# RWKV-7 score products of two heads issued in turn, with a PSUM bank for each head

## The chip, the cores and the metric

The kernel runs as one program on one core of a Trainium2 chip. The metric is the device time of one execution in microseconds (us). The kernel before was run three times; every run of a kernel executes the whole program.

## The reference, cut to what matters

The program is a network of several blocks on one sequence of 512 tokens. The change lies in the third block, in its RWKV-7 branch: 8 heads of 64 channels, whose state is a 64 x 64 matrix per head.

```python
def rwkv7_scan(r, decay, k, v, a, b):
    """S_t = S_{t-1} diag(decay_t) + (S_{t-1} a_t) b_t^T + v_t k_t^T ; y_t = S_t r_t. Inputs (B,T,H,N)."""
    ...
def rwkv7_time_mix(pb, mu, w0, w2, a0, a2, g2, k_k, k_a, r_k, lnx_w, lnx_b):
    ...
    kk = l2_normalize(heads(k * f32(k_k)))
    k = k * (1.0 + (a - 1.0) * f32(k_a))
    r, k, v, a, decay = heads(r), heads(k), heads(v), heads(a), heads(decay)
    y = rwkv7_scan(r, decay, k, v, -kk, kk * a)
    ...
```

## The kernel before, in words

The kernel does not step through the 512 tokens. It cuts them into 4 chunks of 128 and works on a pair of heads at a time (`p` = 0 to 3, heads 2p and 2p + 1). Channels lie on the 128 rows of a tile: the first head of a pair on rows 0 to 63, the second on rows 64 to 127. A pair passes through three functions:

- `rwkv_a` (line 1958) prepares the pair: r, k and v mixed with the token before, the normalized key kk (the norm is the matmul at line 1819, followed by ScalarE at 1820 and 1821 and VectorE at 1822), the gates, and the running sum of the log of the decay (a scan, line 1995, and what follows it to line 2006). It leaves `AR` (kk and r, scaled by the decay, two planes of 512 columns) and `B` and `Kb` (b and k, scaled by its inverse). Three more matmuls stand at its end: line 2024 (the bonus) and lines 2028 and 2029 (the output gate). Each uses the one bank "pa".
- `rwkv_b` (line 2033) makes the scores. For each source (`B`, then `Kb`), head and chunk, one matmul of 64 rows multiplies 128 columns of the source with 2 x 128 columns of `AR`; in all 16 matmuls per pair and 64 in the program, in float32. Two chunks of one head share a PSUM bank of the kind "mx". A copy under a mask (`copy_predicated`, VectorE, line 2047) brings the triangle of both chunks into a tile of zeros, `s8z`. There are two banks of the kind "mx", so at most two such groups are in flight. At its end `rwkv_b` calls `tri_inv` on the tile from `B`.
- `tri_inv` (line 1740) inverts 8 triangular matrices of 128 x 128. Blocks of 16 are done by substitution on VectorE (lines 1756 and 1757, fifteen rounds), VectorE transposes them (`iv_xc`, line 1759; `iv_yc`, line 1761), and TensorE doubles the blocks (from line 1769 on), with sums on VectorE (lines 1780, 1781) and copies on ScalarE (up to line 1812), in "mx" banks too.
- `rwkv_d` (line 2051) runs the recurrence over the four chunks with these scores and the inverse (lines 2066 to 2085), one chunk after another, then a layer norm.

The other branch of the block, a gated delta rule, has functions of the same kind (`gdn_b`, its recurrence at lines 1927 to 1941), which use `tri_inv` and the same banks. Large projections (lines 325 to 327, three matmuls of 512 columns for each 128 x 128 block of weights, which VectorE splits into two parts at line 312 and ScalarE casts at line 310) and transposes by a matmul (line 1830) run through all of it.

The order of the work: a list names the pieces in the order in which they are emitted (`ra0` is `rwkv_a` of pair 0, `gb0` the `gdn_b` of pair 0), each is emitted as if it stood some hundred instructions earlier, by a table of priorities, and a scheduler in the framework then places every instruction on its engine by priority and readiness. It may take instructions of a later piece, or of another line, ahead.

```python
BANKS3 = {"pj": 3, "pa": 1, "mx": 2, "o": 1, "ad": 1}
PR3 = {"a": 0, "b": 400, "d": 500, "s": 300, "p": 150, "t": 300, "u": 0}
MIX3 = ("ra0 rb0 ra1 rd0 ga0 rb1 gb0 rd1 ra2 rb2 gd0 ga1 gb1 rd2 ra3 rb3 gd1 ga2 gb2 rd3 ga3 s0 s1 s2"
```

Of the kernel before, what the change touches and what calls it, by code (L numbers as in the profile page):

```python
# [37 lines left out]
# ---------------------------------------------------------------- host layout  # L38
# [5 lines left out]
def w_cols(w):  # L44
    """[K, C] -> [C/128, 128, K/128, 128]: one block of 128 columns per entry."""
    k, c = w.shape
    return w.reshape(k // P, P, c // P, P).transpose(2, 1, 0, 3)


def w_groups(w, kg, n=256):  # L50
    """[K, C] -> [K/(128 kg), C/n, 128, kg, n]: groups of kg k-tiles, n columns."""
    k, c = w.shape
    return w.reshape(k // (kg * P), kg, P, c // n, n).transpose(0, 3, 2, 1, 4)


def w_rows(w):
    """[K, C] -> [C/512, K/128, 128, 512]"""
    k, c = w.shape
    return w.reshape(k // P, P, c // 512, 512).transpose(2, 0, 1, 3)
# [20 lines left out]
def consts():  # L80
    """Constants that depend on shapes alone, [128, n] float32 each."""
# [9 lines left out]
    # block 2: rows of head h broadcast; causal masks [s, t]; distances [t, s]; compressed blocks [t, c]  # L91
# [25 lines left out]
def w_pick(w, blocks):  # L117
    """columns of w by index lists of 128 (None: a column of zeros) -> [n, 128, K/128, 128]"""
# [9 lines left out]
def layout(i):  # L128
    """numpy arrays of the reference -> arrays as the kernel reads them (moves only)."""
# [37 lines left out]
    w = i["hgrn_w_out"][0]                                           # heads 0-1, 2-5, 6-9, 10-13, 14-15  # L167
# [14 lines left out]
    fm = [rng(128 * m, 128) for m in range(4)]                       # 0: gu  # L182
    fm += [rng(1024 + 128 * m, 128) for m in range(8)]               # 4: mq, 8: mk
    fm += [rng(2560 + 128 * m, 128) for m in range(4)]               # 12: mo
    fm += [ui, uf]                                                   # 16
    fm += heads + [rng(a, 128) for a in (3848, 4104, 3592, 3720)]    # 18: nq, 22: nks, 23: nkw, 24: nkc, 25: nvc
    fm += [rng(4384 + 128 * m, 128) for m in range(24)]              # 26: ga, 34: gb, 42: gc
# [22 lines left out]
    fm = [rng(128 * m, 128) for m in range(16)]                      # 0: q, 4: k, 8: v, 12: z  # L210
    fm += [rng(r0 + 128 * m, 128) for m in range(12)]                # 16: r, 20: k, 24: v
    fm += [rng(r0 + 1536, 128), rng(r0 + 1664, 128), u2]             # 28: w_lo a_lo, 29: g_lo, 30: gates, g_lo
    fm += [rng(3888 + 128 * m, 128) for m in range(16)]              # 31: ga, 39: gb
# [17 lines left out]
# ---------------------------------------------------------------- helpers  # L231
def dview(t, off, dims):
    """A view of tile t with free strides of its own: dims = [[stride, count], ...]."""
# [3 lines left out]
class K:  # L237
# [39 lines left out]
    def banks(self, **n):  # L277
        """share the 8 banks of PSUM out to uses that do not wait for one another"""
# [7 lines left out]
    def tables(self, *after):  # L286
        """exp and ln on the scalar engine again, behind the instructions given, which need others"""
# [8 lines left out]
    def ahead(self, n):  # L296
        """schedule what is emitted inside as if it stood n instructions earlier"""
# [4 lines left out]
    # weights: load one unit and split it exactly into two float32r parts  # L302
# [12 lines left out]
    def split(self, hi, lo, src):  # L315
        """hi + lo = src exactly, both float32r."""
# [3 lines left out]
    def mm3(self, out, wpair, xpair, first, last):  # L320
        """out += w^T x with both operands in two parts (the product of the two low parts is
        below float32's rounding)."""
# [6 lines left out]
    def norms(self):  # L329
        """scratch of the norms below; opened before the work that precedes them"""  # L330
        return self.tc.tile_pool(name="nrm", bufs=2)
# [4 lines left out]
    def sums(self, tile, g=None):  # L336
        """add(k) takes tile k of the finished x into the sums of squares (with g, into those of (x g)^2 too);
        finish() returns the sums over all the channels"""
# [16 lines left out]
    def norm_x(self, pool, sums, A, B, g=None):  # L355
        """hh + hl = rms(x) * A + B; with g, x = rms(x) * g first. The sums of both norms are taken at once:
        mean((x r g)^2) = r^2 mean((x g)^2)."""
# [23 lines left out]
    def final(self, pool, sums, g, out):  # L381
        """out = rms(x) * g"""
# [10 lines left out]
    def mod(self, t, x, r, A, B, k, hi, lo):  # L393
        """hi + lo = x * r * A + B"""
# [5 lines left out]
    def rstd(self, pool, xs, n):  # L400
        """1 / sqrt(mean square over the channels of all tiles + eps)"""
# [14 lines left out]
    def layer_ab(self, ad, g, shift, scale, name):  # L416
        """A = (1 + scale) * g, B = shift of a modulated norm, [128, 8] each"""
# [4 lines left out]
    def softplus_neg_abs(self, out, x, bias=None):  # L422
        """out = log(1 + exp(-|x|))"""
# [8 lines left out]
    def logsig(self, out, x, sp):  # L432
        """out = log sigmoid(x) = min(x, 0) - sp, sp = log(1 + exp(-|x|))"""
# [12 lines left out]
    def silu_vec(self, names):  # L446
        """silu of vectors, side by side: [128, len, 8]."""
# [12 lines left out]
    def ada(self, w, cond, grp, bias, out, pool):  # L460
        """out[:, j, :] = (cond @ w)[block j] + bias for a group of 4 blocks of 128 columns, two conditions.
        cond [128, 4, 8]: the high and then the low parts of both."""
# [19 lines left out]
    def ada_later(self, w, cond, groups, bias, out):  # L482
        """the same for one condition, on the vector engine, in steps that other work takes along"""
# [22 lines left out]
    # ------------------------------------------------------------ block 1, layer 0  # L506
# [10 lines left out]
    def hgrn(self):  # L517
        nc, tc, I = self.nc, self.tc, self.I
        cond = self.cond1 = self.silu_vec(["c", "c_ctx"])
        with ExitStack() as st:  # L520
# [5 lines left out]
            with tc.tile_pool(name="hg_x", bufs=1) as xp, tc.tile_pool(name="hg_ar", bufs=16) as arp:  # L526
# [5 lines left out]
                # shift and scale of channels 0-511, then of the others  # L532
# [1598 lines left out]
```

## Time and profile before

| what | value |
|---|---|
| median of 3 runs | 3515.52 us |
| the runs | 3515.52, 3516.84, 3511.62 us |
| span of the profiled execution | 3510.5 us |
| TensorE busy in that span | 3380.7 us (96%) |
| VectorE busy | 2413.4 us (69%) |
| ScalarE busy | 1802.1 us (51%) |
| records of line 2046 | 128 matmuls, from 2542.1 to 2852.7 us |
| masked copies of line 2047 | 32, from 2544.2 to 2854.2 us |

For the profiled execution the span is known, and no time of its own; the three runs stand 1.1 to 6.3 us above this span. In the trace each float32 matmul is recorded twice, so the 64 matmuls of line 2046 are 128 records. The durations of matmul records are modelled at their end; a distance between two starts is safer. Clock columns give the granted clock of TensorE as a share of 2.4 GHz; 0.50 is 1.2 GHz. A time in a chain of waits is the share of the path, not the length of the instruction.

### The profile page before, as it was taken

To read this page: it belongs to the slowest core of one execution; us is meant where nothing else is said; L and a number is where in the kernel's file an instruction comes from. 1 tells how busy PE (TensorE), PEld (TensorE's weight loads), DVE (VectorE), ACT (ScalarE), POOL (GpSimd) and SP (SyncE) were. 2 spreads that over 40 slices of the span, in tenths; PEclk is the share of its full clock that TensorE was granted. 3 is DMA by queue.
4 is the path that set the end of the run, shared out by engine and by line. 5 is a ranking of instruction groups with operands and counts; after the bars stand their busy time and mean duration, and the time that the engine had idled before them with its cause. 6 is when DMAs were issued, how large, how long until landed. Compare 5 with 4: busy or idle time off the path is not lost.

```text
span 3510.5 us, 50868 instructions
## 1 busy us (share of the span) xinstructions
PE 3380.7 (96%) x20328; PEld 2686.3 (77%) x20328; DVE 2413.4 (69%) x3883; ACT 1802.1 (51%) x3000; POOL 123.6 (4%) x56
## 2 busy tenths in 40 slices
PE   7999999999799999999999999999899999999998
PEld 5888888888577777766787778888667667878887
DVE  6787767787689988466565465554757788565545
ACT  6556556466544565444455543334636556544434
POOL 0000000000132330000000000000000000000000
PEclk9999999999899999999999999999969999999999
DMA  6233323321121122333321235542201111323332
GB/s 224 88 102 95 100 91 100 106 79 55 49 72 61 66 78 95 123 108 108 93 79 58 86 120 180 186 157 96 102 21 45 34 43 37 105 88 96 96 96 84
DMA packets 109663, 325.10 MB, mean 93 GB/s; under 512 B 12721, under 2 KB 13361, under 8 KB 108786
## 3 DMA queue, kind: packets, MB, share of 16 engines
q1 hardware_dynamic: 109170, 321.06, 28.1%
q8 instruction: 160, 2.62, 0.3%
q0 software_dynamic: 256, 0.79, 0.1%
q14 instruction: 77, 0.63, 0.1%
HBM read 315.51 MB, written 6.29 MB: 92 GB/s over the span
## 4 chain that ended last, share of the span: by engine, by line
PE 78%; DVE 15%; ACT 4%; issue 2%; DMA 2%; POOL 0%; SPq 0%; DVEq 0%; ACTq 0%
PE ps_pj L326 19%; PE ps_pj L325 19%; PE ps_pj L327 19%; DVE w_lo L312 2%; DMA ada_raw<-ada_w 2%; DVE iv_m L1756 1%; PE ps_mx L1388 1%; PE ps_pj L1365 1%; PE ps_mx L2046 1%; PE ps_o L1394 1%; ACT w_hi L310 1%; DVE iv_xd L1757 1%; PE ps_ad L496 1%; PE ps_mx L326 1%; DVE cv_ul L318 1%
## 5 line engine op out<-in xcount | busy, mean ns | idle before, releaser
L325 PE MATMUL ps_pj<-hh,w_hi 128*128 128x512 f32 x2344 | 937.4, 401 | 19.8 <-ACT hh L397 18.9
L327 PE MATMUL ps_pj<-hh,w_lo 128*128 128x512 f32 x2344 | 935.0, 399 | 0.0
L326 PE MATMUL ps_pj<-hl,w_hi 128*128 128x512 f32 x2344 | 934.9, 399 | 0.0
L310 ACT CAST w_hi<-w_raw 128x1024 fp32r<-128x1024 f32 (+1 forms) x435 | 454.6, 1045 | 767.4 <-PE ps_pj L326 651.2
L312 DVE TENSOR_TENSOR w_lo<-w_raw,w_hi 128x1024 fp32r<-128x1024 f32 (+1 forms) x387 | 470.2, 1216 | 336.4 <-ACT w_hi L310 330.3
L325 PEld LDWEIGHTS ps_pj<-hh,w_hi 128*128 128x128 f32 x2344 | 445.9, 190 | 127.5 <-ACT hh L397 24.3
L326 PEld LDWEIGHTS ps_pj<-hl,w_hi 128*128 128x128 f32 x2344 | 446.0, 190 | 102.0 <-issue 12.9
L327 PEld LDWEIGHTS ps_pj<-hh,w_lo 128*128 128x128 f32 x2344 | 445.6, 190 | 101.3 <-issue 10.7
L493 DVE SCALAR_TENSOR_TENSOR ada_acc<-ada_raw,sv_t_c,ada_acc 128x512 f32<-128x512 f32 x224 | 167.4, 747 | 50.3 <-DMA ada_raw<-ada_w 48.5
L967 DVE SCALAR_TENSOR_TENSOR xT<-ps_pj,ad,xT 128x512 f32<-128x512 f32 x128 | 95.5, 749 | 153.8 <-PE ps_pj L327 153.3
L312 POOL TENSOR_TENSOR w_lo<-w_raw,w_hi 128x1024 fp32r<-128x1024 f32 x48 | 121.1, 2523 | 1175.5 <-ACT w_hi L310 1175.5
L909 DVE SCALAR_TENSOR_TENSOR ps_mx<-cv_ut,vec,ps_mx 128x448 f32<-128x448 f32 (+3 forms) x192 | 128.3, 669 | 1.9 <-PE ps_mx L327 1.0
L909 DVE SCALAR_TENSOR_TENSOR ps_ad<-cv_ut,vec,ps_ad 128x480 f32<-128x480 f32 (+2 forms) x192 | 128.5, 669 | 1.6 <-ACT ps_ad L898 0.5
L327 PE MATMUL ps_pj<-w_hi,hl 128*128 128x256 f32 x416 | 119.0, 288 | 2.5 <-DVE hl L398 2.5
L325 PE MATMUL ps_pj<-w_hi,hh 128*128 128x256 f32 x416 | 120.3, 290 | 0.8 <-ACT hh L397 0.6
L326 PE MATMUL ps_pj<-w_lo,hh 128*128 128x256 f32 x416 | 120.8, 291 | 0.0
L326 PE MATMUL ps_pj<-m_yl,w_hi 128*128 128x512 f32 x256 | 99.9, 390 | 0.0
L327 PE MATMUL ps_pj<-m_yh,w_lo 128*128 128x512 f32 x256 | 99.6, 389 | 0.0
L325 PE MATMUL ps_pj<-m_yh,w_hi 128*128 128x512 f32 x256 | 99.6, 389 | 0.0
L327 PEld LDWEIGHTS ps_pj<-w_hi,hl 128*128 128x128 f32 x416 | 80.7, 195 | 5.7 <-DVE hl L398 3.2
L325 PEld LDWEIGHTS ps_pj<-w_hi,hh 128*128 128x128 f32 x416 | 80.9, 194 | 3.6 <-ACT hh L397 1.2
L326 PEld LDWEIGHTS ps_pj<-w_lo,hh 128*128 128x128 f32 x416 | 80.8, 194 | 1.5 <-issue 0.7
(786 smaller groups left out, 6513.4 us busy)
## 6 DMA issues: line engine op xcount, KB each, us to landing
ada_raw<-ada_w SPq DMA_DIRECT2D x288, 256.0 KB, 2.8
w_raw<-w_in SPq DMA_DIRECT2D x97, 512.0 KB, 3.2
w_raw<-hgrn_w_in SPq DMA_DIRECT2D x64, 512.0 KB, 3.2
w_raw<-w_mlp SPq DMA_DIRECT2D x64, 512.0 KB, 3.3
w_raw<-conv_w_in SPq DMA_DIRECT2D x48, 512.0 KB, 3.2
w_raw<-w_ffn_in SPq DMA_DIRECT2D x44, 512.0 KB, 3.5
w_raw<-hgrn_w_v SPq DMA_DIRECT2D x16, 512.0 KB, 3.3
w_raw<-hgrn_w_out SPq DMA_DIRECT2D x16, 512.0 KB, 3.2
```

Of the source, the lines that this page charges most:

```text
L310: nc.scalar.copy(hi, raw)
L312: (nc.gpsimd if self.on_pool else nc.vector).tensor_tensor(lo, raw, hi.bitcast(F32), op=ALU.subtract)
L318: self.nc.vector.tensor_tensor(lo, src, hi.bitcast(F32), op=ALU.subtract)
L325: mm(out, wh, xh, start=first, stop=False)
L326: mm(out, wh, xl, start=False, stop=False)
L327: mm(out, wl, xh, start=False, stop=last)
L493: nc.vector.scalar_tensor_tensor(acc, raw, cond[:, k:k + 1], acc, op0=ALU.mult, op1=ALU.add)
L496: nc.tensor.matmul(col[:, b:b + 1], acc[:, 128 * b:128 * b + 128], self.c("ones")[:, 0:1], start=True, stop=True)
L909: stt(o, x, tap(j), o, op0=ALU.mult, op1=ALU.add)
L967: self.nc.vector.scalar_tensor_tensor(self.xT[:, m, :], acc, gate[:, m:m + 1], self.xT[:, m, :], op0=ALU.mult, op1=ALU.add)
L1365: mm(sc[:, :n], q[gs, 128 * i:n], ks[b][gs, 0:n], start=True, stop=True)
L1388: mm(banks[c // 512][:, c % 512:c % 512 + 128], p_[:, off[i] + 128 * s:off[i] + 128 * s + 128], dg[:, i, :], start=True, stop=True)
```

## The change

The loop over heads moves inside the loop over chunks. For a pair of chunks, a bank is taken for each of the two heads; the matmuls then alternate between the heads, and the two masked copies follow. The number of matmuls, of copies and of banks is the same. (Comments that the diff also strips are left out.) From here on the lines of the changed kernel are one or two higher: its matmuls are line 2047, its copies line 2049, and `rwkv_d` stands 2 lines later.

```diff
             o = self.s8z[2 if i else self.niv % 2]
-            for h in range(2):
-                hs = slice(64 * h, 64 * h + 64)
-                for c2 in range(0, 4, 2):
-                    sc = self.bank("mx", [P, 2, 2, P])
-                    for j in range(2):
-                        cs = slice(128 * (c2 + j), 128 * (c2 + j) + 128)
-                        mm(sc[:, j], src[hs, cs], AR[hs, :, cs], start=True, stop=True)
-                    nc.vector.copy_predicated(o[:, 4 * h + c2:4 * h + c2 + 2], self.tri2, sc)
+            for c2 in range(0, 4, 2):
+
+                scs = [self.bank("mx", [P, 2, 2, P]) for _ in range(2)]
+                for j in range(2):
+                    cs = slice(128 * (c2 + j), 128 * (c2 + j) + 128)
+                    for h in range(2):
+                        hs = slice(64 * h, 64 * h + 64)
+                        mm(scs[h][:, j], src[hs, cs], AR[hs, :, cs], start=True, stop=True)
+                for h in range(2):
+                    nc.vector.copy_predicated(o[:, 4 * h + c2:4 * h + c2 + 2], self.tri2, scs[h])
             out.append(o)
```

How the built programs differ follows at three places. In these rows "x2" is two such instructions in a row, and a tile's number tells one buffer from another of the same name: `ps_mx_21123` and `ps_mx_21124` are two banks.

**TensorE, pair 0.** The score products of pair 0 before (`ps_mx` with `rw_B` or `rw_K`, two of one head to a bank), with the matmul of line 2024 among them:

```order
L2046 MATMUL ps_mx_21123<-rw_AR_20927,rw_B_21081 128x256 x2
L2046 MATMUL ps_mx_21127<-rw_AR_20927,rw_B_21081 128x256 x2
L2024 MATMUL ps_pa_21115<-rw_r_21099,cst_b3_20722 128x512
L2046 MATMUL ps_mx_21131<-rw_AR_20927,rw_B_21081 128x256 x2
L2046 MATMUL ps_mx_21135<-rw_AR_20927,rw_B_21081 128x256 x2
L2046 MATMUL ps_mx_21139<-rw_AR_20927,rw_K_21082 128x256 x2
L2046 MATMUL ps_mx_21143<-rw_AR_20927,rw_K_21082 128x256 x2
L2046 MATMUL ps_mx_21147<-rw_AR_20927,rw_K_21082 128x256 x2
L2046 MATMUL ps_mx_21151<-rw_AR_20927,rw_K_21082 128x256 x2
```

and in the changed kernel, from the same instruction on:

```order
L2047 MATMUL ps_mx_21123<-rw_AR_20927,rw_B_21081 128x256
L2047 MATMUL ps_mx_21124<-rw_AR_20927,rw_B_21081 128x256
L2047 MATMUL ps_mx_21123<-rw_AR_20927,rw_B_21081 128x256
L2047 MATMUL ps_mx_21124<-rw_AR_20927,rw_B_21081 128x256
L2024 MATMUL ps_pa_21115<-rw_r_21099,cst_b3_20722 128x512
L2047 MATMUL ps_mx_21131<-rw_AR_20927,rw_B_21081 128x256
L2047 MATMUL ps_mx_21132<-rw_AR_20927,rw_B_21081 128x256
L2047 MATMUL ps_mx_21131<-rw_AR_20927,rw_B_21081 128x256
L2047 MATMUL ps_mx_21132<-rw_AR_20927,rw_B_21081 128x256
L2028 MATMUL ps_pa_21119<-s3_sg1_20862,rw_lw_20925 128x512
```

The two heads now alternate product by product, and lines 2024 and 2028 stand between the groups (line 2029 between the third and the fourth). Behind the last product came, before, the first steps of the recurrence (lines 2066, 2067), the gate and projections, and then the norm of pair 1 (line 1819):

```order
L2066 MATMUL ps_ad_21581<-rw_vt_21113,s8_2_20913 128x64
L2067 MATMUL ps_o_21580<-rw_vt_21113,s8_2_20913 128x64
L2028 MATMUL ps_pa_21119<-s3_sg1_20862,rw_lw_20925 128x512
L2066 MATMUL ps_ad_21581<-rw_vt_21113,s8_2_20913 128x64
L2067 MATMUL ps_o_21580<-rw_vt_21113,s8_2_20913 128x64
L2029 MATMUL ps_pa_21119<-s3_sg2_20780,rw_lw_20925 128x512
L326 MATMUL ps_pj_21717<-hl_92,w_hi_21713 128x512
L327 MATMUL ps_pj_21717<-hh_91,w_lo_21715 128x512
L325 MATMUL ps_pj_21717<-hh_91,w_hi_21713 128x512
L326 MATMUL ps_pj_21717<-hl_92,w_hi_21713 128x512
L1819 MATMUL ps_pa_21494<-rw_sq_21387,cst_b3_20722 128x512
```

and now, from the last group on:

```order
L2047 MATMUL ps_mx_21147<-rw_AR_20927,rw_K_21082 128x256
L2047 MATMUL ps_mx_21148<-rw_AR_20927,rw_K_21082 128x256
L2047 MATMUL ps_mx_21147<-rw_AR_20927,rw_K_21082 128x256
L2047 MATMUL ps_mx_21148<-rw_AR_20927,rw_K_21082 128x256
L2068 MATMUL ps_ad_21581<-rw_vt_21113,s8_2_20913 128x64
L2069 MATMUL ps_o_21580<-rw_vt_21113,s8_2_20913 128x64
L2068 MATMUL ps_ad_21581<-rw_vt_21113,s8_2_20913 128x64
L2069 MATMUL ps_o_21580<-rw_vt_21113,s8_2_20913 128x64
L1819 MATMUL ps_pa_21494<-rw_sq_21387,cst_b3_20722 128x512
L326 MATMUL ps_pj_21717<-hl_92,w_hi_21713 128x512
L327 MATMUL ps_pj_21717<-hh_91,w_lo_21715 128x512
```

The norm of pair 1 comes straight behind the recurrence's first steps, ahead of the projections. From the first score product of pair 0 up to the first matmul of its inverse (line 1769) there were 55 projection matmuls, and now there are 71.

**TensorE, pair 1.** The first score products of pair 1 (`rw_B_21538`), among steps of pair 0's recurrence, before:

```order
L2046 MATMUL ps_mx_21880<-rw_AR_21384,rw_B_21538 128x256
L2066 MATMUL ps_ad_21598<-rw_vt_21113,s8_2_20913 128x64 x2
L2069 MATMUL ps_ad_21598<-ch_S0_20909,rw_AR_20927 128x128
L2070 MATMUL ps_o_21580<-ch_S0_20909,rw_AR_20927 128x128
L2046 MATMUL ps_mx_21880<-rw_AR_21384,rw_B_21538 128x256
L2074 MATMUL ps_ad_21598<-rw_r_21605,iv_Y0_20906 128x64 x2
L2046 MATMUL ps_mx_21884<-rw_AR_21384,rw_B_21538 128x256
L2078 MATMUL ps_ad_21598<-rw_vt_21113,rw_kt_21097 128x128
L2079 MATMUL ps_ad_21598<-rw_u_21609,rw_bt_21090 128x128
L2085 MATMUL ps_o_21580<-rw_u_21609,s8_0_20911 128x64 x2
L2067 MATMUL ps_o_21580<-rw_vt_21113,s8_2_20913 128x64 x2
L2046 MATMUL ps_mx_21884<-rw_AR_21384,rw_B_21538 128x256
```

and now:

```order
L2047 MATMUL ps_mx_21880<-rw_AR_21384,rw_B_21538 128x256 x2
L2076 MATMUL ps_ad_21581<-rw_r_21586,iv_Y0_20906 128x64 x2
L2047 MATMUL ps_mx_21881<-rw_AR_21384,rw_B_21538 128x256
L2080 MATMUL ps_ad_21581<-rw_vt_21113,rw_kt_21097 128x128
L2081 MATMUL ps_ad_21581<-rw_u_21590,rw_bt_21090 128x128
L2087 MATMUL ps_o_21580<-rw_u_21590,s8_0_20911 128x64 x2
L2069 MATMUL ps_o_21580<-rw_vt_21113,s8_2_20913 128x64 x2
L2047 MATMUL ps_mx_21881<-rw_AR_21384,rw_B_21538 128x256
L2047 MATMUL ps_mx_21888<-rw_AR_21384,rw_B_21538 128x256
L2068 MATMUL ps_ad_21598<-rw_vt_21113,s8_2_20913 128x64 x2
L2071 MATMUL ps_ad_21598<-ch_S0_20909,rw_AR_20927 128x128
L2072 MATMUL ps_o_21580<-ch_S0_20909,rw_AR_20927 128x128
```

Here the built order does not alternate product by product: both products of a bank come before those of the other head's bank, and the heads change from bank to bank. In pairs 2 and 3 it is the same: the eight groups of two products stand where they stood, but the first head's group is followed by one of the second head.

**VectorE, the inverse of pair 0.** The end of the substitution (`iv_m`, `iv_xd`) and the two transposes (`iv_xc`, `iv_yc`), with pair 1's scan (`rw_cum`, line 1995) and what follows it, before:

```order
L1756 TENSOR_TENSOR iv_m_21203<-iv_ld_21159,iv_xd_20905 128x450
L434 SCALAR_TENSOR_TENSOR rw_e_21513<-rw_e_21513,rw_s_21517 128x512
L1757 TENSOR_REDUCE iv_xd_20905<-iv_m_21203 128x2x15
L312 TENSOR_TENSOR w_lo_22509<-w_raw_22505,w_hi_22507 128x1024
L1759 STREAM_TRANSPOSE iv_xc_21206<-iv_xd_20905 128x32x32
L1761 STREAM_TRANSPOSE iv_yc_21208<-iv_xd_20905 128x32x32
L1995 SCALAR_TENSOR_TENSOR rw_cum_21523<-cst_g_84,rw_e_21513 128x512
L312 TENSOR_TENSOR w_lo_22543<-w_raw_22539,w_hi_22541 128x1024
L2000 COPY rw_ref_21526<-rw_cum_21523 128x4
L2001 TENSOR_TENSOR rw_sc_21525<-rw_cum_21523,rw_ref_21526 128x3
L2002 TENSOR_TENSOR rw_sc_21525<-rw_sc_21525,rw_ref_21526 128x3
L2005 TENSOR_TENSOR rw_cum_21523<-rw_cum_21523,rw_ref_21526 128x512
```

and now:

```order
L1995 SCALAR_TENSOR_TENSOR rw_cum_21523<-cst_g_84,rw_e_21513 128x512
L1756 TENSOR_TENSOR iv_m_21200<-iv_ld_21159,iv_xd_20905 128x392
L2000 COPY rw_ref_21526<-rw_cum_21523 128x4
L1757 TENSOR_REDUCE iv_xd_20905<-iv_m_21200 128x2x14
L2001 TENSOR_TENSOR rw_sc_21525<-rw_cum_21523,rw_ref_21526 128x3
L312 TENSOR_TENSOR w_lo_22543<-w_raw_22539,w_hi_22541 128x1024
L1756 TENSOR_TENSOR iv_m_21203<-iv_ld_21159,iv_xd_20905 128x450
L2002 TENSOR_TENSOR rw_sc_21525<-rw_sc_21525,rw_ref_21526 128x3
L2005 TENSOR_TENSOR rw_cum_21523<-rw_cum_21523,rw_ref_21526 128x512
L1757 TENSOR_REDUCE iv_xd_20905<-iv_m_21203 128x2x15
L2006 TENSOR_TENSOR rw_e_21513<-rw_cum_21523,rw_e_21513 128x512
L1759 STREAM_TRANSPOSE iv_xc_21206<-iv_xd_20905 128x32x32
```

The scan, the steps behind it up to line 2006 and one weight split (`w_lo_22543`) moved from behind the transposes to ahead of them. Behind them, three products and a mix of pair 1 (lines 2011, 2013, 2014, 1642) now stand ahead of line 1780, and ScalarE has three exponentials and a cast ahead of the copy of the inverse's first doubling.

## Rows read from the trace of the kernel before

**Rows 1.** The page, part 1: busy time of each engine.

```profile
PE 3380.7 (96%) x20328; PEld 2686.3 (77%) x20328; DVE 2413.4 (69%) x3883; ACT 1802.1 (51%) x3000; POOL 123.6 (4%) x56
```

**Rows 2.** Windows: stretch, length, PE, PEld, DVE, ACT, POOL busy (instructions), PE clock, DMA, GB/s.

```profile
2400.00:2420.00 20.00, 20.00 (x90) 16.56 (x89) 6.98 (x7) 10.84 (x16) 0.00 (x0) 1.00 0.29 93
2539.90:2567.20 27.30, 26.51 (x59) 16.55 (x60) 14.88 (x35) 6.87 (x15) 0.54 (x1) 0.50 0.07 26
...
2597.90:2642.30 44.40, 44.40 (x148) 32.03 (x148) 20.86 (x40) 13.27 (x30) 0.00 (x0) 0.50 0.02 9
...
2738.20:2747.60 9.40, 9.01 (x50) 5.86 (x47) 8.56 (x15) 4.80 (x10) 0.00 (x0) 1.00 0.02 7
```

**Rows 3.** Chain of waits, 2539.9 to 2642.3 us: start, us, what.

```profile
2542.21 3.71 PE ps_mx L2046 x8
2545.91 2.00 PE ps_pa L2024 x2
2547.92 9.48 PE ps_mx L2046 x24
2557.40 0.62 PE ps_ad L2066 x2
2558.02 0.43 PE ps_o L2067 x2
...
2565.01 1.72 PE ps_pa L1819 x2
...
2580.38 2.02 DVE iv_xc L1759
...
2604.55 1.15 PE ps_mx L2046 x2
...
2613.79 1.16 PE ps_mx L2046 x4
...
2616.95 2.00 PE ps_mx L2046 x4
```

**Rows 4.** TensorE's timeline at pair 0: start, us, instruction.

```profile
2550.74 0.79 PE L2046 MATMUL ps_mx<-rw_AR,rw_K 64*128 64x256 f32 x1
2551.00 0.63 PE L2046 MATMUL ps_mx<-rw_AR,rw_B 64*128 64x256 f32 x1
```

**Rows 5.** TensorE's timeline at pair 2.

```profile
2738.25 1.13 PE L2046 MATMUL ps_mx<-rw_AR,rw_B 64*128 64x256 f32 x4
2739.31 0.44 PE L1830 MATMUL ps_pa<-cst_g,rw_v 128*128 128x128 f32 x2
2739.68 1.65 PE L2046 MATMUL ps_mx<-rw_AR,rw_B 64*128 64x256 f32 x8
2741.26 0.66 PE L1927 MATMUL ps_ad<-gd_vt,iv_Y 128*128 128x64 f32 x4
```

**Rows 6.** TensorE's timeline at pair 3.

```profile
2843.88 1.99 PE L2046 MATMUL ps_mx<-rw_AR,rw_B 64*128 64x256 f32 x8
2845.80 0.43 PE L1927 MATMUL ps_ad<-gd_vt,iv_Y 128*128 128x64 f32 x2
```

**Rows 7.** The instructions of line 2047: ns min/median/max, first and last start.

```profile
L2047 DVE COPY_PREDICATED s<-tri_u,ps_mx x32: 704/725/756, 2544.2 to 2854.2; 128x512 f32<-128x512 uint8 x32
```

**Rows 8.** VectorE's waits, 2556 to 2582 us: us in total, times, longest.

```profile
DVE rw_kk L1822 <- ACT rw_sq L1821: 5.2, 1, 5.2
```

**Rows 9.** ScalarE's timeline: an exponential and a cast.

```profile
2842.77 0.61 ACT L1491 ACTIVATE si_e<-si_e 128x512 f32<-128x512 f32 x1
...
2844.48 1.03 ACT L310 CAST w_hi<-w_raw 128x1024 fp32r<-128x1024 f32 x1
```

**Rows 10.** VectorE's timeline behind the transposes of pair 0's inverse.

```profile
2584.06 1.18 DVE L1995 TENSOR_TENSOR_SCAN rw_cum<-cst_g,rw_e 128x512 f32<-128x512 f32 x1
...
2586.75 0.68 DVE L2005 TENSOR_TENSOR rw_cum<-rw_cum,rw_ref 128x512 f32<-128x512 f32 x1
2587.35 0.41 DVE L1780 TENSOR_TENSOR iv_yy<-iv_yc,ps_mx 128x256 f32<-128x256 f32 x1
```

## The prediction, made before the changed kernel had run

> **What bounds the kernel now.** I read the busy line of the page first: TensorE is busy in 3380.7 of 3510.5 us, VectorE in 2413.4 [rows 1]. So time that TensorE wins counts, unless the stretch in which it is won ends on another engine. The run times stand above this one profiled span: their median, 3515.5 us, is 5.0 above 3510.5. The sum below is made against the span and carried over by that difference. About 0.2% (7.0 us) is what a measurement of this kernel can tell from no change.
>
> Then the windows: around the score products of the first pair, and through those of the second, TensorE was granted 0.50 of its clock, which is 1.2 GHz, with 26.51 of 27.30 and 44.40 of 44.40 us busy; the projections before (90 records in 20.00 us) and the third pair ran at 1.00 [rows 2]. The same product therefore has two prices, and pairs 0 and 1 pay the high one.
>
> Third, the chain of waits shows that at pairs 0 and 1 these products set the end: they lie on it piece after piece, and between them only other TensorE work [rows 3]. Pair 0 pays 3.71 us for 8 records and 9.48 for 24, that is 13.19 for its sixteen products (a product shows as two records). Pair 1 mixes them singly among the steps of the recurrence of pair 0.
>
> Fourth, the TensorE timelines. They answer what the change asks: do two heads on different row halves run at once? A K record of head 0 starts at 2550.74 and lasts 0.79, while the last B record of head 1, earlier in the program, starts only at 2551.00 [rows 4]. In pair 2 two products of head 0 take from 2738.25 to 2739.31, 1.06 us; the neighbouring groups of head 0 and head 1, four products, take from 2739.68 to 2741.26, 1.58 and not 2.1 [rows 5]. So records of the two halves stream side by side, already before the change, wherever a product of one head follows one of the other.
>
> **The prices at half clock**, from [rows 3]: a pair of products of one head, alone between other work, 2.00 us (4 records); a single one 1.15; a pair across the heads 1.16. From 3.71 for 8 records and 2.00 for 4 a further record costs (3.71 - 2.00) / 4 = 0.43; so two records in a stream would be 0.86, and a single visit pays 0.29 more for entering and leaving.
>
> That extra 0.29 is what the Trainium skill (TensorEngine Tiling, Key Properties) calls the drain when the tiling mode changes, and it speaks against cutting pair 0's products into more groups. By it a stretch pays once per visit, as the rows show; without it four groups would cost 1.2 us less than I count.
>
> **The change part by part.** The number of products (64), of their columns and of the masked copies (32) stays; only order and banks move.
>
> *Pair 0.* The order shows true alternation here: head 0, head 1, head 0, head 1 into two banks, four times, with the three 2.00 us matmuls of lines 2024, 2028 and 2029 between. In a group each head has two products, and the heads stream side by side, so I price a group like the pair of one head: 2.00. Four groups are 8.0 in place of 13.19: **-5.2 us**. The bounds: no overlap at all gives four groups of 8 records at 3.71, 14.8, so +1.6; overlap with everything in a stream and no extra for visits gives four times 1.71, 6.8, so -6.4. I stay with 2.00, since the overlap stands in [rows 4]. The two copies behind each group take 0.725 us each [rows 7], 1.45 in all, and the matmul between takes 2.00 at half clock: they hide; if the clock rose there, that cover would be 1.0, and about 0.45 would show three times. The same three matmuls were issued before as well; they only move.
>
> The Trainium skill (TensorE: Matmul & The Clock Gate, section "Part 3: Packing small matmuls — row/col tiling") says that matmuls start and end in the order of the program. The trace disagrees in one place: the K record at 2550.74 starts ahead of the earlier B record at 2551.00 [rows 4]. By that rule a group would last one record longer, 2.43, the pair would win 3.5 instead of 5.2, and the time would be 3510.5.
>
> *Pair 1.* The order shows that the alternation is not kept: the scheduler places both products of one bank together, and heads alternate only from group to group. Before, I count eight singles, one pair across the heads and three pairs of one head: 8 x 1.15 + 1.16 + 3 x 2.00 = 16.36. After, two pairs of one head, three across, six singles: 2 x 2.00 + 3 x 1.16 + 6 x 1.15 = 14.4. **-2.0 us**; bounds 0 (if the neighbours do not meet, since steps of the recurrence come between) and -2.5.
>
> *Pair 2.* Here, at full clock, a pair of head 1 followed one of head 0 directly and took 1.58 with it; now each of the first three groups stands between other work, with one neighbour of the other head fewer. I take two separate groups, 1.06 + 1.06: **+0.5**. *Pair 3*: two groups of head 0 in a row take 2843.88 to 2845.80, 1.92 [rows 6]; now they are of both heads, 1.58 if side by side, 2.1 if the second bank is late, as it comes free only when ScalarE has copied the inverse out: **-0.1**, bounds -0.3 and +0.2. The K products of both pairs already met the other head or do so as before: 0.
>
> *What is moved with it.* At pair 0 the norm of pair 1 (line 1819) comes straight behind the score products instead of among the projections. It ended at 2565.01 + 1.72 = 2566.7; now at 2542.1 + 8.0 + 3 x 2.0 + 2 x 1.05 (lines 2068 and 2069, 0.62 + 0.43) + 2.0 = 2560.2. VectorE had waited 5.2 us for what follows from it [rows 8]: that wait should shrink to almost nothing. In its place VectorE becomes the engine that is late: the inverse of pair 0 runs on it. I cost this at nothing beyond the -5.2, since TensorE has projections to do meanwhile: sixteen more of them now stand ahead of the inverse's first matmul, 16 x 20.00 / 90 = 3.6 us [rows 2].
>
> **Sum**: -5.2 - 2.0 + 0.5 - 0.1 = -6.8; the profiled span would be 3503.7, the time 3515.5 - 6.8 = **3508.7 us**, 0.19% faster, at the edge of what can be told.
>
> **The rivals.**
> (a) *More: the clock rises.* If the two streams bring the grant to 1.00 after the first group and the first 2.00 us matmul, the remaining 14.1 of the 18.1 us up to the end of line 1819 halve: -7.0 more, 3501.7. For it: the clock did return to 1.00 by pair 2. Against: it stayed at 0.50 with TensorE busy 26.51 of 27.30 and 44.40 of 44.40 us [rows 2], and no row shows two heads streaming for long. 0.18.
> (b) *Hidden.* Pair 0's gain is eaten, because not these products but the chain on VectorE to the inverse ends the stretch (the transpose at 2580.38 [rows 3]), and TensorE then waits there. Then only pairs 1 to 3 count, -1.6: 3513.9. For it: the chain leaves TensorE right behind line 1819 and stays with VectorE to 2584. Against: line 1819, where it leaves, comes 6.5 us earlier. 0.18.
> (c) *Slower: the inverse is pushed back.* In the new order VectorE does pair 1's scan and what follows it (lines 1995 to 2006) and one split of a weight before the inverse's transpose instead of after it. From 2584.06 to 2587.35 these take 3.29, with line 2006 of the size of line 2005 (0.68) 4.0 [rows 10]; three products and a mix of that size (4 x 0.68 = 2.7) go ahead of the next step; on ScalarE three exponentials and a cast do, by rows of such work 3 x 0.61 + 1.03 = 2.9 [rows 9]. If all stand on the path and pair 0's gain does not, it is -1.6 + 9.6 = +8.0: 3523.5. It decides if the transpose starts later than 2580.38. For it: VectorE's own queue is in this order, whatever is late. Against: work done earlier is not done later, pair 1's path wins it back, and VectorE had 5.2 us of waiting to put it in [rows 8]. 0.16.
> (d) *It doesn't do what it says.* For pairs 1 to 3 this is so by the order, and the forecast has it; for pair 0 it is excluded.
>
> **How the numbers follow.** Forecast 0.48, (a) 0.18, (b) 0.18, (c) 0.16. The forecast lies at the bound, so half of it is faster by over 0.2%: faster 0.24 + 0.18 = 0.42, same 0.24 + 0.18 = 0.42, slower 0.16. The forecast's own range, by its bounds and the rule on order above, is 3506 to 3513. The range of all takes in that, (b) and half of (a) and (c): from 3499 (2.7 below (a), as fewer projections then run at half clock) to 3521.
>
> **What would show it.** Right: pair 0's products in four groups of about 2.0 us, records of the two heads with nearly the same start; VectorE's 5.2 us wait gone; line 1819 ending some 6 us earlier; the transpose no later than 2580. Wrong: groups of 3.7 (no overlap), a window of pair 0 at a clock other than 0.50, a transpose that starts at 2583 or later, or TensorE waiting there for VectorE where it did not. Should the stages after pair 3 take another time than before, my sum, which ends there, has missed it.

## The result: faster by 0.77%, four times what was forecast

| | before | changed |
|---|---|---|
| median | 3516.18 us (8 runs, 3492.91 to 3524.52) | 3492.09 us (8 runs, 3479.11 to 3498.44) |
| ratio, with its 95% interval | | 0.9923 [0.9904, 0.9943] |
| span of the profiled execution | 3510.5 us | 3482.4 us |
| mean granted clock in it | 0.974 | 0.983 |

The sign was the forecast one, the size was not: 27 us by the ratio (24 by the medians), where 6.8 were forecast, and the median lies under the stated range (3499 to 3521). The busy line of the page of the changed kernel, which answers to [rows 1], holds the first hint:

```profile
PE 3350.4 (96%) x20328; PEld 2665.7 (77%) x20328; DVE 2414.5 (69%) x3883; ACT 1801.9 (52%) x3000; POOL 123.8 (4%) x56
```

TensorE does the same instructions in 30.3 us less, and VectorE and ScalarE take what they took. Nothing was left out, so TensorE ran faster. The windows of pair 0 (from its first score product, over 25.1 us) and of pair 1 (from its first to its last) say where; the columns are those of [rows 2], with the granted clock in the third place from the end.

```profile
2546.90:2572.00 25.10, 25.10 (x104) 16.02 (x104) 22.00 (x48) 13.71 (x24) 0.54 (x1) 0.94 0.09 27
2592.20:2595.40 3.20, 3.20 (x37) 2.65 (x36) 0.00 (x0) 2.44 (x5) 0.00 (x0) 1.00 0.00 0
2595.40:2612.10 16.70, 16.70 (x102) 12.41 (x101) 12.40 (x21) 8.28 (x18) 0.00 (x0) 1.00 0.00 1
```

Before, the same two stretches, 25.1 and 33.1 us long, had:

```profile
2542.10:2567.20 25.10, 25.10 (x55) 15.52 (x55) 12.70 (x30) 4.98 (x11) 0.54 (x1) 0.50 0.03 8
2595.90:2599.50 3.60, 2.93 (x34) 2.65 (x33) 0.92 (x2) 3.07 (x6) 0.00 (x0) 0.78 0.41 146
2604.50:2637.60 33.10, 33.10 (x100) 23.18 (x100) 12.82 (x21) 8.06 (x19) 0.00 (x0) 0.50 0.00 1
```

Pair 0 went from 0.50 to 0.94 and pair 1 from 0.50 to 1.00, its products from 33.1 to 16.7 us. The middle line is the last step of pair 0's inverse, just ahead of pair 1; it will matter. The TensorE timeline of the changed kernel at pair 0, which answers to [rows 3, 4]:

```profile
2546.88 2.08 PE L2047 MATMUL ps_mx<-rw_AR,rw_B 64*128 64x256 f32 x8
2548.88 1.55 PE L2024 MATMUL ps_pa<-rw_r,cst_b 128*128 128x512 f32 x2
2550.36 1.14 PE L2047 MATMUL ps_mx<-rw_AR,rw_B 64*128 64x256 f32 x8
2551.43 1.12 PE L2028 MATMUL ps_pa<-s_sg,rw_lw 128*128 128x512 f32 x2
...
2557.05 1.08 PE L1819 MATMUL ps_pa<-rw_sq,cst_b 128*128 128x512 f32 x2
```

The first group of four products (8 records) takes 2.00 us from its start to the start of line 2024, still at half clock; the second, at full clock, 1.07. So the two heads do stream side by side, and at the price that was set. The norm of pair 1 (line 1819) ends at 2558.1, 11.2 us after the first product; before it was 24.6 us after it (2542.1 to 2566.7).

### The profile page after: what moved, and what is told of

The parts are those of the page before. It is cut to its first block, busy times and chain, and to the rows that moved or that the text cites. A ratio compares the mean times of both kernels' runs of the same rounds, so it can differ in the third digit from the quotient of the medians.

```text
span 3482.4 us, 50868 instructions
## 1 busy us (share of the span) xinstructions
PE 3350.4 (96%) x20328; PEld 2665.7 (77%) x20328; DVE 2414.5 (69%) x3883; ACT 1801.9 (52%) x3000; POOL 123.8 (4%) x56
## 4 chain that ended last, share of the span: by engine, by line
PE 78%; DVE 14%; ACT 4%; DMA 2%; issue 2%; POOL 0%; DVEq 0%; SPq 0%; ACTq 0%
PE ps_pj L325 19%; PE ps_pj L326 19%; PE ps_pj L327 19%; DVE w_lo L312 2%; DMA ada_raw<-ada_w 1%; DVE iv_m L1756 1%; PE ps_mx L1388 1%; PE ps_pj L1365 1%; PE ps_o L1394 1%; ACT w_hi L310 1%; PE ps_ad L496 1%; DVE iv_xd L1757 1%; PE ps_mx L326 1%; DVE cv_ul L318 1%; PE ps_mx L2047 1%
```

## Where the 28 us of the two profiles lie

Both programs are the same up to pair 0, but their executions reach it 4.8 us apart. So I count, in us, from the first score product of pair 0, in every profile of this study. "Transpose" is the start of line 1759, in pair 0's inverse and in the inverse after it. The last two columns are the granted clock in the windows of the two pairs.

| profile | transpose 1 | pair 1 begins | transpose 2 | last matmul | clock, pair 0 | clock, pair 1 |
|---|---|---|---|---|---|---|
| before | 38.3 | 62.4 | 123.4 | 957.9 | 0.50 | 0.50 |
| changed | 31.3 | 48.5 | 93.9 | 925.0 | 0.94 | 1.00 |
| changed, once more | 32.1 | 52.8 | 113.5 | 944.8 | 0.91 | 0.50 |
| changed order at pair 0 alone | 31.1 | 47.9 | 94.1 | 923.7 | 0.97 | 1.00 |
| the same, once more | 32.2 | 52.9 | 114.4 | 944.6 | 0.90 | 0.52 |
| changed order at pairs 1 to 3 alone | 38.3 | 62.5 | 123.2 | 962.4 | 0.50 | 0.50 |
| a bank per head, products in pairs | 27.9 | 49.8 | 110.2 | 947.0 | 0.94 | 0.50 |
| before, one matmul more | 38.2 | 60.5 | 104.1 | 948.7 | 0.50 | 1.00 |
| before, two matmuls more | 38.2 | 59.3 | 107.3 | 964.3 | 0.50 | 1.00 |
| a bank per head, two matmuls more | 28.6 | 47.7 | 95.4 | 920.7 | 0.91 | 1.00 |
| a bank per head, one matmul more | 27.9 | 48.1 | 90.9 | 942.4 | 0.94 | 1.00 |
| before, once more | 38.3 | 61.0 | 122.5 | 961.5 | 0.50 | 0.50 |
| changed, a longer wait | 32.3 | 56.0 | 100.2 | 938.5 | 0.90 | 1.00 |
| changed, in program order | 32.1 | 89.0 | 119.4 | 1001.6 | 0.91 | 1.00 |

Of 32.9 us between the first two rows, 13.9 are won by the time pair 1 begins, 15.6 more up to the second transpose, 3.6 up to the third, and nothing behind it. The rest of the table is the work of the experiments. The theory that they were to test, **E** (entry): pair 0 is paid by its two heads side by side, which bring the clock back; pair 1 is paid by the clock at which TensorE comes to it, which is settled at the end of pair 0's inverse. Its rivals: **O** (overlap), that pair 1's own products of two heads bring its clock back; and **C** (chance), that the clock falls out differently in every execution of any kernel.

## The experiments

### Which pair's order pays

Pair 0 alone in the changed order:

```diff
-            for c2 in range(0, 4, 2):
+            if p == 0:
+                for c2 in range(0, 4, 2):
...
+            else:
+                for h in range(2):
```

> Pair 0 issues its products in the changed order, pairs 1 to 3 in the old one. Theory E (entry): what pays is that TensorE comes to pair 1 at a granted clock of 1.00, because of the order around pair 0 and its inverse; then this kernel wins about what the whole change wins, a ratio of 0.990 to 0.995 to before, and its window of pair 1's products shows 1.00. Theory O (overlap in pair 1): what pays is that the products of pair 1 meet the other head; then this one wins only pair 0's 5 us, a ratio of 0.998 to 1.000, and pair 1 runs at 0.50. Theory C (chance): the clock of pair 1 falls out differently from execution to execution in every kernel; then the single times spread over 30 us or more in this kernel as in the others.

Measured: 3479.1 us, ratio 0.9888 [0.9866, 0.9910], four times between 3476 and 3482. All of the gain is there with the old order in pairs 1 to 3, and pair 1 ran at full clock:

```profile
2545.70:2570.80 25.10, 25.10 (x105) 16.25 (x105) 21.65 (x47) 13.89 (x24) 0.54 (x1) 0.97 0.09 28
2593.60:2613.40 19.80, 19.80 (x117) 14.31 (x116) 14.92 (x25) 9.35 (x22) 0.00 (x0) 1.00 0.00 1
```

So O is false as the cause. The other half of the edit, pairs 1 to 3 alone (against the kernel above):

```diff
-            if p == 0:
+            if p > 0:
```

> Pair 0 issues its products in the old order, pairs 1 to 3 in the changed one; the order around pair 0's inverse is that of before. Theory E: pair 1 is entered at 0.50 as before and stays there, ratio 0.998 to 1.002. Theory O: pair 1 runs at 1.00, ratio 0.990 to 0.995. Theory C: as for the kernel with pair 0 alone.

Measured: 3516.6 us, ratio 0.9995 [0.9975, 1.0015]. Both pairs at half clock, and pair 1 took 32.7 us where it had taken 33.1:

```profile
2549.00:2574.10 25.10, 25.10 (x55) 15.51 (x55) 12.73 (x30) 4.97 (x11) 0.54 (x1) 0.50 0.02 8
2611.50:2644.20 32.70, 32.70 (x100) 22.40 (x100) 12.73 (x21) 8.03 (x19) 0.00 (x0) 0.50 0.00 1
```

In pair 1 the steps of the recurrence stand between most of the products, so that a product seldom has one of the other head for a neighbour, whatever the loop says.

A bank per head, but both products of a head together:

```diff
-                for j in range(2):
-                    cs = slice(128 * (c2 + j), 128 * (c2 + j) + 128)
-                    for h in range(2):
-                        hs = slice(64 * h, 64 * h + 64)
+                for h in range(2):
+                    hs = slice(64 * h, 64 * h + 64)
+                    for j in range(2):
+                        cs = slice(128 * (c2 + j), 128 * (c2 + j) + 128)
```

> All pairs take a bank per head in turn, but both products of a head are issued together, so nothing alternates product by product; the order around pair 0's inverse is that of before. Theory E: pair 0's products take about 13 us at half clock still or somewhat less where two heads' groups touch, pair 1 stays at 0.50, ratio 0.998 to 1.001. Theory O: what pair 1 has of neighbours of two heads is about what the changed kernel has, so ratio 0.990 to 0.995.

Measured: 3500.7 us, ratio 0.9955 [0.9934, 0.9977]. Neither theory foretold the whole of it, and it splits the gain in two: pair 0 at 0.94, pair 1 at 0.50.

```profile
2545.50:2570.60 25.10, 23.95 (x94) 15.01 (x94) 22.00 (x48) 12.55 (x22) 0.54 (x1) 0.94 0.03 9
2595.30:2626.80 31.50, 31.50 (x101) 21.88 (x100) 12.78 (x21) 8.20 (x19) 0.00 (x0) 0.50 0.00 1
```

```profile
2545.55 2.09 PE L2047 MATMUL ps_mx<-rw_AR,rw_B 64*128 64x256 f32 x8
2547.56 1.52 PE L2024 MATMUL ps_pa<-rw_r,cst_b 128*128 128x512 f32 x2
2549.01 1.17 PE L2047 MATMUL ps_mx<-rw_AR,rw_B 64*128 64x256 f32 x8
```

The first two groups, two products of head 0 and then two of head 1, take the 2.01 us of the alternating order at half clock. Product by product is not needed: it is enough that the group behind is of the other head. Before, the groups came as head 0, head 0, then head 1, head 1. On VectorE and ScalarE the order of instructions is that of before, and on TensorE, but for the heads, one instruction stands elsewhere: the first matmul of the gate (line 2028), by three places. So the order of the heads is what brought pair 0's clock back. All profiles of the table agree: the five with the old order at pair 0 show 0.50 there, the nine with the heads in turn 0.90 to 0.97.

The kernel before, once more:

> The kernel before, profiled once more. Theories E and O: pair 1's window shows 0.50 again, from about 2598 to 2642 us, ratio 1.000 within 0.002. Theory C: pair 1's window may show 1.00 this time and the span is then some 20 us shorter.

Measured: 3513.1 us, ratio 0.9989 [0.9971, 1.0007]; both pairs at half clock again.

```profile
2539.70:2564.80 25.10, 25.10 (x55) 15.49 (x55) 12.69 (x30) 4.97 (x11) 0.54 (x1) 0.50 0.03 8
2600.70:2633.80 33.10, 33.10 (x100) 23.18 (x100) 12.85 (x21) 8.05 (x19) 0.00 (x0) 0.50 0.00 1
```

### Is it chance?

The changed kernel and the kernel with pair 0 alone, both again, on one chip:

> The changed kernel once more. Its eight times lie in two heaps, 3479 to 3484 and 3491 to 3498 us, with mean clocks of 0.983 to 0.984 and 0.977 to 0.980. Theory E: the second heap are executions in which one stretch, pair 1's or an inverse's, falls to 0.50 for some 25 us; a profile of such an execution shows which. Theory N (noise spread over the whole program): no such stretch, the low stretches are the same ones, a little longer each.

> Pair 0 alone in the changed order, beside the changed kernel on the same chip. If its four times of 3476 to 3482 us were what this kernel does, it is 0.99 of before and some 0.3% under the changed kernel, whose times lie in two heaps; if they were chance, some of its times now lie at 3490 to 3500 us too and the two kernels are the same within 0.2%.

Measured: 3493.6 us (3481.6 to 3514.9), ratio 0.9935 [0.9912, 0.9958], and 3482.5 us (3474.5 to 3506.0), ratio 0.9926 [0.9899, 0.9952]. The second kernel's eleven times lie in two heaps, six from 3474.5 to 3482.5 and five from 3497.8 to 3506.0; its first four times, on another chip, were all of the lower heap. The two kernels are the same within the noise. The changed kernel's twelve times are not two heaps: three of them, 3510.8 to 3514.9 us, lie where the kernel before lies, and no profile shows what those executions had. Both profiles happened to be executions with pair 1 at half clock. For the changed kernel, the whole low stretch (so theory N is out for this execution) and pair 1 in it:

```profile
2574.50:2625.70 51.20, 50.36 (x357) 37.26 (x358) 24.18 (x42) 18.81 (x41) 0.00 (x0) 0.50 0.03 11
2592.00:2622.70 30.70, 30.70 (x103) 22.18 (x101) 12.94 (x21) 8.28 (x18) 0.00 (x0) 0.50 0.00 1
```

One and the same program takes 45.4 us (93.9 - 48.5) from pair 1's first product to the second transpose, or 60.7 (113.5 - 52.8). That is C's share: the order does not settle pair 1's clock. Of the four profiles of these two kernels, two have pair 1 at full clock; in the two profiles of the kernel before, and in the one of the kernel with pairs 1 to 3 alone, pair 1 is at 0.50. The kernel before is not wholly without the faster course either: of its 92 timed executions three took 3492.1 to 3498.5 us, and no profile here is of one of those.

### What acts on the clock of pair 1

At the end of pair 0's inverse the kernel before has this on TensorE, just ahead of pair 1:

```profile
2595.92 1.14 PE L1806 MATMUL ps_mx<-iv_x,s 64*64 64x64 f32 x16
2597.74 1.83 PE L1811 MATMUL ps_mx<-iv_Y,iv_x 64*64 64x64 f32 x16 [0.67 <-ACT iv_x L1808]
```

and the changed kernel, whose scheduler let projections in there:

```profile
2592.17 1.14 PE L1806 MATMUL ps_mx<-iv_x,s 64*64 64x64 f32 x16
2593.24 0.50 PE L325 MATMUL ps_pj<-hh,w_hi 128*128 128x512 f32 x1
2593.58 0.39 PE L326 MATMUL ps_pj<-hl,w_hi 128*128 128x512 f32 x1
2593.81 0.40 PE L327 MATMUL ps_pj<-hh,w_lo 128*128 128x512 f32 x1
2594.04 0.39 PE L325 MATMUL ps_pj<-hh,w_hi 128*128 128x512 f32 x1
2594.36 1.14 PE L1811 MATMUL ps_mx<-iv_Y,iv_x 64*64 64x64 f32 x16
```

In the first TensorE waits 0.67 us ahead of line 1811; the granted clock fell to 0.50 at 2597.9, just behind that wait, and stayed there for 44.4 us. So I put work into that place of the kernel before, first two matmuls and then one:

```diff
+        if self.niv == 1:
+            pr = self.tc.cur_priority
+            for _ in range(1):
+                mm(ps, self.c("ident"), Y[:, 0:4, :], start=True, stop=True)
+            self.tc.cur_priority = pr
         for hc in range(8):
             mm(ps[u, hc, :], b[l, hc, :], Y[l, hc, l], start=True, stop=True)
```

> The kernel before with one more matmul (128 rows, 512 columns, its result overwritten by the next) between lines 1806 and 1811 of pair 0's inverse, 0.9 us of work at full clock, partly in a gap of 0.67; every other instruction stands in the order of before on all engines. Theory E: it decides at which clock pair 1 is entered, so in at least some executions pair 1 runs at 1.00 and the time is some 16 us lower; a median of 3497 to 3505 us, or two heaps some 16 us apart. If one matmul is too little, or where the clock stood at pair 1 is not decided there: as before within 2 us, 3514 to 3519.

Measured: 3505.6 us (3488.6 to 3528.7), ratio 0.9969 [0.9950, 0.9987], 0.6 us above the median that E gave. It is faster, with one matmul more and nothing else moved. The matmul (line 1813) takes the place of the wait:

```profile
2593.12 1.14 PE L1806 MATMUL ps_mx<-iv_x,s 64*64 64x64 f32 x16
2594.20 1.12 PE L1813 MATMUL ps_mx<-iv_Y,cst_g 128*128 128x512 f32 x2
2595.25 1.14 PE L1816 MATMUL ps_mx<-iv_Y,iv_x 64*64 64x64 f32 x16
```

```profile
2539.30:2564.40 25.10, 25.10 (x55) 15.56 (x55) 12.67 (x30) 4.96 (x11) 0.54 (x1) 0.50 0.02 8
2599.80:2617.80 18.00, 18.00 (x100) 12.98 (x100) 13.28 (x22) 7.59 (x19) 0.00 (x0) 1.00 0.00 1
2875.20:2895.70 20.50, 20.50 (x58) 14.41 (x57) 8.61 (x21) 5.94 (x18) 0.00 (x0) 0.50 0.00 0
```

Pair 0 stays at 0.50, as it should; pair 1 runs at 1.00, in 18.0 us where it took 33.1, and the second transpose comes 19.3 us earlier (123.4 to 104.1). The third line tells why the whole kernel won only 9 us in this execution: a later stretch fell to half clock for 20.5 us. Its times are spread, not in two clean heaps, so the 16 us forecast for single executions can't be read from the times; from the profile they can.

This wait is not the only place where the clock of pair 1 is decided. In the second profile of the kernel before, the clock fell 1.2 us ahead of the same wait (line 1811 starts at 2593.8 there), and stayed low through pair 1:

```profile
2591.90:2639.70 47.80, 47.13 (x164) 34.28 (x163) 22.11 (x44) 15.46 (x34) 0.00 (x0) 0.50 0.04 11
```

In the changed kernel the clock fell earlier still, behind TensorE's wait of 3.6 to 3.7 us for pair 0's transpose. In the first profile it fell at 2580.5 and was back at 2590.7, ahead of the projections shown above; in the second it fell at 2574.5 and did not come back, and these projections and all of pair 1 then ran at 0.50 (the window from 2574.5 in the section on chance). So one matmul in the place of the wait can keep the clock up; what brings it back ahead of that place, in some executions and not in others, stays open.

With two matmuls:

> The kernel before, scores untouched, with two more matmuls of 128 rows and 512 columns at the end of pair 0's inverse, between lines 1806 and 1811, whose result is overwritten by line 1811. Behind them the scheduler places some later work differently, so this is not the filler alone. Theory E: TensorE comes to pair 1 at 1.00 and stays there; pair 1's stretch of 44 us halves, and in spite of some 2 us of added work the kernel is 15 to 25 us faster, a ratio of 0.993 to 0.996; pair 0 stays at 0.50 for some 27 us. Theory O (only products of two heads side by side keep the clock up): pair 1 stays at 0.50, ratio 1.000 to 1.003.

Measured: 3520.6 us (3492.8 to 3530.1), ratio 0.9990 [0.9964, 1.0015]: a miss on the time. Five times lie from 3492.8 to 3499.0, seven from 3518.7 to 3530.1, and the profile is of the upper heap. Pair 1 does run at 1.00, but the scheduler placed later work otherwise, and a stretch around the fourth inverse sits at half clock for 54.7 us:

```profile
2548.50:2573.60 25.10, 25.10 (x55) 15.55 (x55) 12.67 (x30) 4.96 (x11) 0.54 (x1) 0.50 0.03 8
2607.80:2627.60 19.80, 19.80 (x119) 14.85 (x118) 14.11 (x25) 8.00 (x20) 0.00 (x0) 1.00 0.01 1
2764.90:2819.60 54.70, 54.70 (x252) 39.33 (x252) 18.66 (x51) 18.71 (x44) 0.00 (x0) 0.50 0.05 15
```

The two matmuls and the one, with a bank per head:

> A bank per head in turn with both products of a head issued together (which brought pair 0 to 1.00 in the look before and left pair 1 at 0.50), and the same two matmuls at the end of pair 0's inverse. Theory E: both pairs at 1.00, ratio 0.987 to 0.993 to before. Theory O: as without the two matmuls or some 2 us more, ratio 0.995 to 0.998.

> A bank per head in turn, both products of a head together, and the one matmul at the end of pair 0's inverse: on all engines the order of the kernel with the banks alone and this one instruction more. That kernel has 3500.7 us with pair 1 at 0.50. Theory E: pair 1 at 1.00 in at least some executions, 3480 to 3488 in those; else as without it, 3500 within 3.

Measured: 3476.2 us (five times, 3474.3 to 3482.3), ratio 0.9891 [0.9872, 0.9911], and 3488.6 us (3477.1 to 3494.9), ratio 0.9917 [0.9900, 0.9933]. Both pairs at full clock in both:

```profile
2546.70:2571.80 25.10, 23.92 (x91) 14.53 (x91) 20.79 (x46) 12.25 (x22) 0.54 (x1) 0.91 0.03 8
2594.40:2611.80 17.40, 17.40 (x105) 12.80 (x104) 13.28 (x23) 6.92 (x17) 0.00 (x0) 1.00 0.00 1
```

```profile
2539.70:2564.80 25.10, 23.92 (x94) 14.95 (x94) 21.98 (x48) 12.56 (x22) 0.54 (x1) 0.94 0.04 11
2587.80:2605.00 17.20, 17.20 (x100) 12.28 (x100) 13.24 (x22) 7.62 (x19) 0.00 (x0) 1.00 0.00 1
2952.30:2979.60 27.30, 27.19 (x341) 21.90 (x342) 11.35 (x25) 11.62 (x23) 0.00 (x0) 0.50 0.12 40
```

Against the banks alone (3500.7 us) that is 24 and 12 us for matmuls that compute nothing wanted. With one matmul, every other instruction stands in the order of the kernel with the banks alone; with two, later work is placed otherwise here too. The profile with one (the last line) has 27.3 us at half clock in the last of the program's eight inverses, and its time, 3494.5 us, lies above the 3480 to 3488 that E gave. The kernel with two has the lowest median here, below the changed one measured beside it (0.9891 [0.9872, 0.9911] against 0.9935 [0.9912, 0.9958]); five runs don't exclude a second heap.

The same with work that is wanted, by a longer wait that the scheduler fills with projections:

```diff
         nc.scalar.copy(b[l], ps[l])
+        if self.niv == 1:
+            pr = self.tc.cur_priority
+            for _ in range(3):
+                nc.scalar.copy(b[l], ps[l])
+            self.tc.cur_priority = pr
```

> The changed kernel with three more copies on ScalarE ahead of line 1811 in pair 0's inverse (each repeats the copy of line 1808, some 0.6 us): the scheduler puts 14 projections in place of 4 between lines 1806 and 1811, work that is done anyway. Theory E: pair 1 is entered at 1.00 in every execution, one heap at 3475 to 3484 us, a ratio of 0.988 to 0.991 to before. Otherwise two heaps as in the changed kernel, or, if the wait itself costs more than it wins, 3495 or above.

Measured: 3491.8 us (3480.1 to 3496.7), ratio 0.9924 [0.9908, 0.9940], no better than the changed kernel. Pair 1 is at 1.00 in the profile, but pair 1 begins 56.0 us after pair 0, 7.5 later than in the first profile of the changed kernel, and a stretch behind it fell to half clock:

```profile
2601.50:2619.00 17.50, 17.50 (x106) 13.15 (x106) 13.11 (x22) 8.83 (x19) 0.00 (x0) 1.00 0.09 31
2748.40:2775.70 27.30, 27.19 (x328) 20.95 (x324) 9.46 (x23) 7.67 (x17) 0.00 (x0) 0.50 0.06 21
```

Whether every execution entered pair 1 at full clock can't be seen from six times; it stays open.

### Alternation in every pair

```diff
-                        mm(scs[h][:, j], src[hs, cs], AR[hs, :, cs], start=True, stop=True)
+                        m = mm(scs[h][:, j], src[hs, cs], AR[hs, :, cs], start=True, stop=True)
+                        if p:
+                            self.tc.keep_in_program_order(m)
```

> The changed kernel with pairs 1 to 3 held to the order of the program as well, so that the heads alternate product by product in every pair. If the products of pair 1 side by side matter by themselves, it is 2 to 6 us under the changed kernel's best heap (3474 to 3480 us); if not, its heaps lie where those of the changed kernel lie. Holding the order lets fewer projections through between the products, so a pair may start later: then it is slower, 3500 us or more.

Measured: 3545.5 us, ratio 1.0073 [1.0049, 1.0098], slower than before. Pair 1's products take only 9.5 us, but they begin 89.0 us after pair 0's, and TensorE has gaps later:

```profile
2631.30:2640.80 9.50, 9.35 (x45) 5.38 (x44) 6.71 (x8) 6.15 (x11) 0.00 (x0) 1.00 0.16 55
2796.00:2847.20 51.20, 45.00 (x148) 33.42 (x148) 28.46 (x71) 20.90 (x48) 0.00 (x0) 0.50 0.03 11
```

So holding every pair to the alternation cost more than it was worth: 6.2 us idle in one stretch of 51.2, all of it at half clock.

## Why the prediction was wrong, step by step

- **What bounds the kernel**: right. Pairs 0 and 1 are bound by TensorE: of the 16.4 us that pair 1's products won, 15.6 reached the next transpose.
- **The price of a group at pair 0, 2.00 us at half clock**: right, 2.00 measured. The rule of the Trainium skill (TensorE: Matmul & The Clock Gate, section "Part 3: Packing small matmuls — row/col tiling") that matmuls start in program order would have made it 2.43; the trace does not bear it out here either.
- **The step that failed: that pairs 0 and 1 "pay the high one" of the two prices in the changed kernel too.** The forecast held the clock fixed at what [rows 2] showed. At pair 0 it rose after the first group, as rival (a) had it: the norm of pair 1 ended 11.2 us after the first product, where the forecast had 18.1 and (a) 11.1. (a) got 0.18 because the clock had stayed low with TensorE busy all the time [rows 2]; but busy, at pair 0, with products of one head after another, and just that the change took away. At pair 1 the higher clock made of the term of -2.0 one of -16.4 in the first profile (33.1 to 16.7 us), where TensorE came to it at 1.00. And (a) itself was priced too small, since it carried the clock no further than line 1819. Pair 1's stretch, 15 to 16 us, was in no case of mine.
- **Pair 1, -2.0**: within its bounds, where the clock was the one it was priced for. In the profiles with pair 1 at 0.50 its products take 30.7 us (the changed kernel), 31.5 (a bank per head) and 32.7 (pairs 1 to 3 alone) against 33.1. **Pair 2, +0.5, and pair 3, -0.1**: from first to last product 9.8 against 9.0 us, and 8.7 against 8.8; right in sign, small in sum.
- **VectorE's wait of 5.2 us at line 1822** [rows 8] was to go, and went. The waits of VectorE in the changed kernel from pair 0 to the transpose:

```profile
DVE s L2049 <- PE ps_mx L2047: 2.3, 3, 1.1
DVE rw_bon L2025 <- PE ps_pa L2024: 0.2, 1, 0.2
```

- **Rivals (b) and (c)**: their mechanism is there, but not enough. Of 13.4 us that TensorE won up to line 1819, 7.0 reached the transpose (38.3 to 31.3), in part since pair 1's scan and what follows it now stand on the path ahead of it. The chain of waits of the changed kernel:

```profile
2571.86 1.13 DVE rw_cum L1995
...
2574.45 1.13 DVE w_lo L312
...
2576.57 0.60 DVE rw_cum L2005
...
2577.71 0.60 DVE rw_e L2006
2578.31 2.00 DVE iv_xc L1759
```

  These are 3.5 us, of the 4.0 that (c) counted; the kernel with the banks alone, whose VectorE order is that of before, reaches the transpose 3.4 us earlier (27.9). TensorE waits 3.7 us for the transpose, by its list of waits, and 1.4 before. But the work was not added: pair 1 began 13.9 us earlier, more than the 13.4.
- **Rival (d)**: excluded for pair 0, as said; for pairs 1 to 3, where the change does not do what it says, its own worth is nil (0.9995).

## What to carry to other kernels

Two heads on two halves of the rows need no alternation product by product, with two products to a group as here: it is enough that neighbours in TensorE's queue lie on different halves, which an order of the groups gives. Before a term is priced by a row at half clock, ask whether the change takes away the work that ran while the clock was low, and follow the clock on to the next stretches; a stretch that is entered low can stay low with TensorE busy all the time. Where a program has such stretches, time it many times and read the clock of each profile, as one profile shows one of several courses.

## What was not expected of the hardware

The clock with which a stretch begins can last through it: the same products of pair 1, with TensorE busy for every microsecond of both windows, ran at 1.00 for 16.7 us in one execution and at 0.50 for 30.7 in another of the same program. One matmul of 1.05 us (2594.20 to 2595.25) ahead of them moved the kernel before from 3515.7 to 3505.6 us. What was not tried is to hold the course of the clock itself, so the share of executions that enter pair 1 at full clock is not known, nor why later stretches fall in some executions and not in others.
